# Strassen's seven products for the gate and up projections of a hybrid decoder layer's two FFNs, and the down projection in three batches

## Chip, core and metric

The kernel runs on one core of one Trainium2 chip. The metric is device time in microseconds (us): the median over runs of the whole program. PE is TensorE, DVE is VectorE, ACT is ScalarE, POOL is GpSimd, SP is the engine whose queue issues most DMAs.

## What is computed

One inference step of a layer over 544 tokens (512 prompt rows and 8 x 4 sample rows), width 1024, all in fp32:

```
x += 0.5 * SwiGLU_1(rms(x))            # gate,up: 1024 -> 2 x 2816, down: 2816 -> 1024
h  = rms(x); u = h @ w_in              # mixer: windowed attention and gated DeltaNet
x += merged(attention, deltanet) @ w_out
x += 0.5 * SwiGLU_2(rms(x))
y  = rms(x)
def _swiglu(x, w_gu, w_down):
    gate, up = jnp.split(x @ w_gu, 2, axis=-1)
    return (jax.nn.silu(gate) * up) @ w_down
```

## The kernel before

Channels lie on the partitions, tokens along the free axis, in two halves of 272 (`sl(0)`, `sl(1)`). A product of two fp32 matrices is made of three matmuls of rounded parts: every operand is kept as hi (rounded) and lo (the rest), and `unit` issues hi x hi, hi x lo and lo x hi for each of the 8 tiles of the contraction, 24 matmuls of 128x128 by 128x272 into one PSUM accumulator.

The program is built by Python: `make_plan` writes the list of units, `kernel_units` goes through it. For each unit it calls `prefetch` (which brings weight tiles in), the unit's own function (its matmuls), and then the unit's `evac` (what DVE, ACT and POOL make of the accumulator). Every engine works through its own queue in the order of issue.

An FFN has 22 slices of 128 hidden channels. A slice costs four units: gate (`u_g`) and up (`u_u`) for two token halves, 96 matmuls. `u_g`'s evac multiplies by 1/rms (`R(h)`) on DVE and takes a tanh on ACT; `u_u`'s evac makes silu(gate) * up with three more DVE operations and splits it into `hh` hi (ACT) and lo (DVE). After 11 slices comes a batch of 16 down units (`u_d`, 33 matmuls each) whose evac adds to the residual `x`; then 11 more slices and 16 more down units.

Weights arrive in chunks of 8 tiles (`raw`, 512 KB, SP queue), are split in groups of four tiles (128x512) into hi by ACT and lo by a DVE subtraction (`split_next`; in the mixer the subtraction is mostly POOL's). Outside the mixer there are 8 + 4 such groups (`G2`, `G`), so three slices' worth can be ready ahead. The norm: `xw_tile` multiplies x by the norm's weight and splits it (`xh`, `xl`), `norm_acc` sums squares on POOL, `norm_fin` makes 1/rms on DVE, which is applied after the products.

Of the kernel before, what the change touches and what calls it, by code (L numbers as in the profile page):

```python
# [10 lines left out]
F32 = mybir.dt.float32  # L11
# [14 lines left out]
FB = 11  # L26
# [99 lines left out]
class Plan:  # L126
    """Order in which the 128 x 128 weight tiles are used; host and chip follow it."""
# [16 lines left out]
def stagger(n, tail, head=0):  # L144
    """(tile, half) order: the first `head` and the last `tail` tiles go half by half."""
    out = [(i, h) for h in range(2) for i in range(head)]
    for i in range(head, n - tail):
        out += [(i, 0), (i, 1)]
    out += [(i, h) for h in range(2) for i in range(n - tail, n)]
    return out  # L150


def make_plan():
    pl = Plan()
    units = []

    def ffn(which):
        gu, dn = f"w_ffn{which}_gu", f"w_ffn{which}_down"
        for b in range(2):
            order = stagger(FB, 0, 2 if b == 0 else 0) if (which, b) != (1, 0) else stagger(FB, 2, 2)  # L160
            for f, h in order:
                f += b * FB
                units.append(("g", which, f, h, pl.col(gu, range(KT), f * P)))
                units.append(("u", which, f, h, pl.col(gu, range(KT), (FT + f) * P)))
            for n, h in stagger(KT, 0 if b == 0 else 2 if which == 1 else 4):
                units.append(("d", which, b, n, h, pl.col(dn, range(b * FB, b * FB + FB), n * P)))

# [36 lines left out]
def consts():  # L204
    """Arrays that depend on shapes alone: identity, masks and distances."""
# [53 lines left out]
class Builder:  # L259
    def __init__(self, tc, nc, A, pl, units, cp, sp, pp, dp):  # L260
# [5 lines left out]
        self.next_group = 0  # L266
        self.next_raw = self.top = 0
        self.side = []
        self.due, self.rings = {}, {}
        self.last = False  # L270
        self.busy = set()
        self.nps = 0
        self.in_mix = False
        self.plan_groups()
# [15 lines left out]
    def until(self, ok):  # L290
        """The side chains go on until something holds."""
# [57 lines left out]
    def mm_ps(self):  # L349
        self.nps += 1  # L350
        if not self.in_mix and self.nps % 8 > 2:
            return self.sd_ps()
# [28 lines left out]
    def mm(self, out, lhsT, rhs, start=True, stop=True):  # L381
        return self.nc.tensor.matmul(out, lhsT, rhs, start=start, stop=stop)
# [5 lines left out]
    def rsqrt(self, out, v, tmp, steps):  # L388
        """out = v ** -0.5 by a shifted exponent and Newton steps."""
# [3 lines left out]
        for k in range(steps):  # L393
            a, b = (-0.703952253, 0.703952253 * 2.38924456) if k == 0 else (-0.5, 1.5)
            self.tt(tmp, out, out, ALU.mult)
            self.stt(tmp, tmp, a, v, ALU.mult, ALU.mult)
            self.stt(out, tmp, b, out, ALU.add, ALU.mult)
            yield "vector"

# [1 line left out]
    def load_raw(self, upto):  # L401
        nch = self.A["in_W_dram"].shape[0]
        while self.next_raw <= min(upto, nch - 1):
            c = self.next_raw
            pool, tag, bufs = self.sp, "raw", CFG["RAW"]
            if c % 3 == 2 and not self.in_mix and c * CHUNK // GRP not in self.resident:
                pool, tag, bufs = self.mp, "raw2", 1
# [5 lines left out]
    def plan_groups(self):  # L413
        self.last_use, self.resident = {}, set()
        first_pa = next(i for i, u in enumerate(self.units) if u[0] == "pa")
        first_ba = next(i for i, u in enumerate(self.units) if u[0] == "ba")
        for i, u in enumerate(self.units):
            for t in u[-1]:
                self.last_use[t // GRP] = i
                if first_ba <= i < first_pa:  # L420
                    self.resident.add(t // GRP)
        self.held = {"G": [], "G2": []}

    def split_next(self, ui, pool=None):
        """Bring the next group of weight tiles in as hi + lo if a slot is free."""
        k = self.next_group
        c = k * GRP // CHUNK
        for tag, bufs in (("G2", CFG["G2"]), ("G", CFG["G"])):
            if tag == "G2" and (k in self.resident or self.in_mix):
                continue  # L430
            self.held[tag] = [g for g in self.held[tag] if self.last_use[g] >= ui]
            if len(self.held[tag]) < bufs:
                break
# [1360 lines left out]
```

## Time and profile before

| | |
|---|---|
| median of 3 runs | 1734.03 us (1730.92 to 1737.05) |
| profiled execution, span | 1730.2 us |
| PE / DVE / ACT / POOL busy | 1656.1 / 1072.3 / 573.1 / 373.4 us |
| mean granted TensorE clock | 0.983 |
| first FFN, mixer, second FFN (about) | 8 to 415, 415 to 1285, 1317 to 1717 us |

Busy times are unions of the recorded spans of an engine. A matmul's own span (288 ns) overlaps those of its neighbours, so the cost of one is its pitch, not its span. The median is 3.8 us above the profiled span.

### The profile page before, as it was taken

To read this page: it belongs to the slowest core of one execution; us is meant where nothing else is said; L and a number is where in the kernel's file an instruction comes from. 1 tells how busy PE (TensorE), PEld (TensorE's weight loads), DVE (VectorE), ACT (ScalarE), POOL (GpSimd) and SP (SyncE) were. 2 spreads that over 40 slices of the span, in tenths; PEclk is the share of its full clock that TensorE was granted. 3 is DMA by queue.
4 is the path that set the end of the run, shared out by engine and by line. 5 is a ranking of instruction groups with operands and counts; after the bars stand their busy time and mean duration, and the time that the engine had idled before them with its cause. 6 is when DMAs were issued, how large, how long until landed. Compare 5 with 4: busy or idle time off the path is not lost.

```text
span 1730.2 us, 33573 instructions
## 1 busy us (share of the span) xinstructions
PE 1656.1 (96%) x13373; PEld 1607.8 (93%) x13373; DVE 1072.3 (62%) x2508; ACT 573.1 (33%) x1356; POOL 373.4 (22%) x441
## 2 busy tenths in 40 slices
PE   8999999999988999999899899999999999999997
PEld 7999999999988888888889788999999999999996
DVE  7754255545879869789958665344456654255534
ACT  5332223332332324343333244333233323223332
POOL 5000000011545534454425233420011000000012
PEclk9999999999999999999999999999999999999999
DMA  5223222322333455446347666332243222223221
GB/s 177 87 85 98 86 86 86 98 85 75 111 100 115 135 180 185 135 156 193 117 137 238 171 219 182 123 119 89 86 139 97 84 89 87 97 74 98 86 75 63
DMA packets 116434, 205.13 MB, mean 119 GB/s; under 512 B 30962, under 2 KB 57108, under 8 KB 116276
## 3 DMA queue, kind: packets, MB, share of 16 engines
q1 hardware_dynamic: 104708, 162.43, 29.2%
q0 software_dynamic: 10992, 39.99, 7.7%
q8 instruction: 105, 1.72, 0.4%
q10 hardware_dynamic: 576, 0.56, 0.1%
q14 instruction: 53, 0.43, 0.1%
HBM read 172.20 MB, written 30.73 MB: 117 GB/s over the span
## 4 chain that ended last, share of the span: by engine, by line
PE 73%; DVE 20%; DMA 3%; ACT 2%; issue 2%; SPq 1%; POOL 0%; DVEq 0%; ACTq 0%
PE sd L120 40%; PE mm L120 32%; DVE y L120 4%; DVE Yc L120 3%; DVE inv L120 2%; DVE H L120 1%; DVE nrm L120 1%; DVE ast L120 1%; DVE av L120 1%; DVE s L120 1%; DVE R L120 1%; DMA md<-ast 1%; DVE U L120 1%; DVE kq L120 1%; DVE r L120 1%
## 5 line engine op out<-in xcount | busy, mean ns | idle before, releaser
L120 PE MATMUL mm<-xh,G 128*128 128x272 f32 x3632 | 753.7, 297 | 21.6 <-DVE smp L120 10.4
L120 PEld LDWEIGHTS mm<-xh,G 128*128 128x128 f32 x3632 | 596.6, 192 | 42.5 <-issue 26.5
L120 PE MATMUL mm<-xl,G 128*128 128x272 f32 x1816 | 530.0, 292 | 0.5 <-DVE xl L120 0.4
L120 PE MATMUL sd<-xh,G 128*128 128x272 f32 x1904 | 363.4, 288 | 0.0
L120 PEld LDWEIGHTS mm<-xl,G 128*128 128x128 f32 x1816 | 349.2, 192 | 1.4 <-DVE xl L120 0.6
L120 ACT ACTIVATE G<-raw 128x512 fp32r<-128x512 f32 x474 | 273.3, 619 | 178.6 <-PE mm L120 111.6
L120 PEld LDWEIGHTS sd<-xh,G 128*128 128x128 f32 x1904 | 300.5, 188 | 0.2
L120 POOL TENSOR_TENSOR G<-raw,G 128x512 fp32r<-128x512 f32 x158 | 217.3, 1391 | 322.7 <-ACT G L120 303.0
L120 PE MATMUL sd<-xl,G 128*128 128x272 f32 x952 | 273.8, 288 | 0.0
L120 DVE TENSOR_TENSOR G<-raw,G 128x512 fp32r<-128x512 f32 x316 | 204.7, 690 | 70.9 <-ACT G L120 66.7
L120 POOL TENSOR_TENSOR acc<-acc,H 128x272 f32<-128x272 f32 x55 | 44.7, 814 | 911.5 <-ACT H L120 908.1
L120 PEld LDWEIGHTS sd<-xl,G 128*128 128x128 f32 x952 | 179.0, 188 | 0.1
L120 PE MATMUL sd<-hh,G 128*128 128x272 f32 x1287 | 163.0, 288 | 0.0
L120 PEld LDWEIGHTS sd<-hh,G 128*128 128x128 f32 x1287 | 161.8, 188 | 0.1
L120 ACT ACTIVATE H<-H 128x272 f32<-128x272 f32 (+1 forms) x105 | 45.1, 429 | 193.4 <-DVE H L120 193.4
L120 ACT ACTIVATE hh<-H 128x272 fp32r<-128x272 f32 x88 | 38.0, 431 | 202.0 <-DVE H L120 202.0
L120 PE MATMUL mm<-hh,G 128*128 128x272 f32 x825 | 104.7, 288 | 0.0
L120 PEld LDWEIGHTS mm<-hh,G 128*128 128x128 f32 x825 | 103.8, 188 | 0.0
L120 DVE SCALAR_TENSOR_TENSOR y<-U,vec,y 128x568 f32<-128x568 f32 x72 | 94.2, 1308 | 7.8 <-ACT y L120 6.0
L120 DVE SCALAR_TENSOR_TENSOR H<-H,H 128x272 f32<-128x272 f32 x120 | 55.2, 460 | 26.3 <-ACT H L120 25.8
L120 DVE SCALAR_TENSOR_TENSOR x<-sd,x 128x272 f32<-128x272 f32 x49 | 21.4, 439 | 77.9 <-PE sd L120 77.9
L120 DVE TENSOR_TENSOR hh<-H,hh 128x272 fp32r<-128x272 f32 x88 | 38.9, 442 | 43.8 <-ACT hh L120 43.8
(257 smaller groups left out, 1853.3 us busy)
## 6 DMA issues: line engine op xcount, KB each, us to landing
raw<-in_W_dram SPq DMA_DIRECT2D x161, 512.0 KB, 3.6
raw<-in_W_dram POOLq DMA_DIRECT2D x76, 512.0 KB, 4.0
qkv<-qd SPq DMA_DIRECT2D x36, 256.0 KB, 5.4
st<-in_ssm_dram SPq DMA_DIRECT2D x32, 256.0 KB, 4.5
cache<-in_kc_dram SPq DMA_DIRECT2D x28, 256.0 KB, 5.2
cache<-in_vc_dram SPq DMA_DIRECT2D x28, 256.0 KB, 4.3
qd<-av SPq DMA_DIRECT2D x24, 256.0 KB, 4.2
out_dram<-av SPq DMA_DIRECT2D x24, 256.0 KB, 3.8
```

The costliest lines, as they stand in the source:

```text
L120: r = f(*args, **kw)
```

## The change

Slices 0 to 3 of the first FFN and 0 to 2 of the second stay as they were. The other 18 + 19 = 37 slices are computed as a 2 x 2 x 2 block product: gate and up are the block rows (A1, A2), the lower and upper four contraction tiles the inner blocks, the two token halves the block columns. Seven products (`PROD`; units `"w"`) of four contraction tiles each replace the eight: 7 x 12 = 84 matmuls. Two pairs of them and one triple accumulate in one bank each, and a product's partial sum is read out of the bank before the next product adds to it.

For that, POOL makes four weight sums of 128x512 per slice (`sums`), and four combinations of the blocks of x (T1 to T4, four tiles each) are made once per FFN (`tset`, on DVE, ACT and POOL). Weights are now split in 1024-wide jobs (sums too), 3 x 1024 + 512 columns per slice instead of 4 x 512; all those subtractions are DVE's. 1/rms is no longer multiplied into up, but into the down product. The hidden value is split for both halves at once (544 wide), lo by POOL except in a batch's last slice. Down runs in batches of 8, 7 and 7 slices; its evac multiplies by 1/rms on DVE and adds to x on POOL (DVE in the last batch).

```diff
+PROD = {1: ("A11", "B11", "A", True), 2: ("A12", "B21", "A", False), 6: ("S2", "T2", "B", True), 7: ("S3", "T3", "B", False),
+        4: ("A22", "T4", "B", False), 5: ("S1", "T1", "C", True), 3: ("S4", "B22", "C", False)}
+FBS = (8, 7, 7)
+NC = {1: 4, 2: 3}
...
+            for f in range(max(f0, nc), f0 + n):
+                if (f, 1) not in begun:
+                    w(f, 1)
+                if f > max(f0, nc):
+                    w(f - 1, 4)
+                last = f == f0 + n - 1
+                w(f, *[p for p in (6, 5, 2, 7) + (() if last else (3,)) if (f, p) not in begun])
+            if f + 1 < FT:
+                w(f + 1, 1)
+            w(f, 3, 4)
+            if f + 1 < FT:
+                w(f + 1, 2, 6, 5)
...
+    def sums(self, j):
...
+        if k[0] == "12":
+            self.tt(t[:, h[1]], y[:, h[0]], y[:, h[1]], ALU.add, pg)
+            self.tt(t[:, h[0]], t[:, h[1]], x[:, h[0]], ALU.add, pg)
+            self.s2 = t
+        else:
+            self.tt(t[:, h[0]], x[:, h[0]], y[:, h[1]], ALU.add, pg)
+            self.tt(t[:, h[1]], x[:, h[1]], self.s2[:, h[0]], ALU.add, pg)
...
+    def u_w(self, which, f, p, wids):
...
+            if p == 1:
+                e["p1"] = self.H()
+                self.act(e["p1"], ps, AF.Copy)
+            elif p == 6:
+                e["V"] = self.H()
+                self.tt(e["V"], ps, e["p1"], ALU.subtract)
+            elif p == 5:
+                e["p5"] = self.H()
+                self.act(e["p5"], ps, AF.Copy)
+            elif p == 2:
+                e["g"] = self.S(name="g")
+                self.tt(e["g"][:, h0], ps, self.R(0), ALU.mult)
...
+            elif p == 7:
+                u3 = self.H()
+                self.tt(u3, ps, e["p1"], ALU.subtract)
+                e["u"] = self.S(name="u")
+                self.tt(e["u"][:, h1], u3, e.pop("p5"), ALU.subtract, pg)
+            elif p == 3:
+                t, g = self.H(), e["g"]
+                self.tt(t, ps, e.pop("V"), ALU.subtract)
+                self.tt(g[:, h1], t, self.R(1), ALU.mult)
+                e["t"] = self.S(name="t")
+                self.act(e["t"], g, AF.Tanh, scale=0.5)
+                self.stt(e["t"], e["t"], 1.0, g, ALU.add, ALU.mult)
...
+            else:
+                t, u = e["t"], e["u"]
+                self.tt(u[:, h0], ps, e["p1"], ALU.subtract)
+                self.tt(t, t, u, ALU.mult)
+                self.h[f] = tuple(self.S(dt=F32R, name="hh") for k in range(2))
+                self.split(*self.h[f], t, None if f + 1 in (FBS[0], FBS[0] + FBS[1], FT) else pg)
```

The order on DVE for one slice of the old kind, slice 4 of the first FFN (G<-raw are the lo halves of weights, H and hh the evacuations of gate and up, two halves one after the other):

```order
L120 TENSOR_TENSOR G_797<-raw_568,G_797 128x512
L120 TENSOR_TENSOR G_800<-raw_568,G_800 128x512
L120 TENSOR_TENSOR H_830<-sd_805,r_361 128x272
L120 TENSOR_TENSOR G_834<-raw_667,G_834 128x512
L120 TENSOR_TENSOR G_837<-raw_667,G_837 128x512
L120 SCALAR_TENSOR_TENSOR H_831<-H_831,H_830 128x272
L120 TENSOR_TENSOR H_831<-H_831,r_361 128x272
L120 TENSOR_TENSOR H_831<-H_831,sd_842 128x272
L120 TENSOR_TENSOR hh_868<-H_831,hh_867 128x272
```

The second half follows with five more such operations and no weights. In the change a slice of the new kind (slice 9) has these twelve on DVE, in the order of the products 6, 2, (weights), 7, (weights), 3, (weights of the slice after next), 4:

```order
L130 TENSOR_TENSOR H_2041<-sd_2028,H_2002 128x272
L130 TENSOR_TENSOR g_2072<-mm_1989,r_363 128x272
L130 TENSOR_TENSOR G_2058<-sw_1942,G_2058 128x1024
L130 TENSOR_TENSOR H_2092<-sd_2028,H_2002 128x272
L130 TENSOR_TENSOR G_2078<-sw_1984,G_2078 128x1024
L130 TENSOR_TENSOR H_2111<-sd_2043,H_2041 128x272
L130 TENSOR_TENSOR g_2072<-H_2111,r_492 128x272
L130 SCALAR_TENSOR_TENSOR t_2114<-t_2114,g_2072 128x544
L130 TENSOR_TENSOR G_2120<-raw_1964,G_2120 128x1024
L130 TENSOR_TENSOR u_2094<-sd_2028,H_2002 128x272
L130 TENSOR_TENSOR t_2114<-t_2114,u_2094 128x544
L130 TENSOR_TENSOR G_2138<-raw_1881,G_2138 128x512
```

Seven of the twelve read two tiles in SBUF; five read an accumulator (sd, mm). On POOL, which had nothing to do in this stretch before, the same slice now has these six (sw are the weight sums for slice 11, two slices ahead):

```order
L130 TENSOR_TENSOR sw_2075<-raw_2026 128x512
L130 TENSOR_TENSOR sw_2075<-sw_2075,raw_1964 128x512
L130 TENSOR_TENSOR u_2094<-H_2092,H_2056 128x272
L130 TENSOR_TENSOR sw_2117<-raw_1964,raw_2026 128x512
L130 TENSOR_TENSOR sw_2117<-raw_1964,sw_2075 128x512
L130 TENSOR_TENSOR hh_2155<-t_2114,hh_2154 128x544
```

POOL's work moved from none to six operations a slice. At the start of the first FFN the lo halves of the third slice's weights stood on POOL before, right behind the sums of squares:

```order
L120 TENSOR_TENSOR acc_216<-acc_216,H_236 128x272
L120 TENSOR_TENSOR G_316<-raw_154,G_316 128x512
L120 TENSOR_TENSOR G_319<-raw_154,G_319 128x512
L120 TENSOR_TENSOR G_324<-raw_175,G_324 128x512
L120 TENSOR_TENSOR G_327<-raw_175,G_327 128x512
```

Now they stand on DVE, behind the evacuations of the first two slices and four operations that make half-sums of x (yt):

```order
L130 TENSOR_TENSOR H_384<-H_384,sd_324 128x272
L130 TENSOR_TENSOR hh_388<-H_384,hh_387 128x272
L130 TENSOR_SCALAR yt_445<-x_73,vec_79 128x272
L130 SCALAR_TENSOR_TENSOR yt_445<-x_73,vec_79,yt_445 128x272
L130 TENSOR_SCALAR yt_450<-x_74,vec_79 128x272
L130 SCALAR_TENSOR_TENSOR yt_450<-x_74,vec_79,yt_450 128x272
L130 TENSOR_TENSOR G_418<-raw_159,G_418 128x1024
L130 TENSOR_TENSOR G_458<-raw_172,G_458 128x1024
```

Those weights moved from an engine that was otherwise free of evacuations into the queue that has them.

## Rows read from the trace of the kernel before

**Rows 1.** The page: span, and busy time of each engine (share, instructions).

```profile
span 1730.2 us, 33573 instructions
PE 1656.1 (96%) x13373; PEld 1607.8 (93%) x13373; DVE 1072.3 (62%) x2508; ACT 573.1 (33%) x1356; POOL 373.4 (22%) x441
```

**Rows 2.** Windows: us, then PE, PEld, DVE, ACT, POOL busy, PEclk, DMA, GB/s.

```profile
8.07:150.80 142.73, 138.38 (x1062) 136.94 (x1063) 96.78 (x182) 53.51 (x118) 21.20 (x20) 0.98 0.33 108
150.80:216.80 66.00, 66.00 (x530) 66.00 (x529) 20.79 (x39) 14.82 (x25) 0.00 (x0) 1.00 0.28 89
216.80:349.10 132.30, 132.30 (x1059) 132.30 (x1058) 75.46 (x153) 40.50 (x85) 0.00 (x0) 1.00 0.28 88
415.00:1285.00 870.00, 816.80 (x6759) 772.74 (x6759) 614.66 (x1615) 298.52 (x787) 318.18 (x373) 0.97 0.46 146
1486.00:1620.00 134.00, 134.00 (x1070) 134.00 (x1069) 67.46 (x136) 37.63 (x76) 0.00 (x0) 1.00 0.29 91
```

**Rows 3.** Chain of work that ended last, one of its longest pieces: start, us, what.

```profile
66.66 15.04 PE sd L120 x120
```

**Rows 4.** Groups by form: busy us, mean ns of one, idle before.

```profile
L120 DVE TENSOR_TENSOR G<-raw,G 128x512 fp32r<-128x512 f32 x316 | 204.7, 690 | 70.9 <-ACT G L120 66.7
L120 DVE TENSOR_TENSOR hh<-H,hh 128x272 fp32r<-128x272 f32 x88 | 38.9, 442 | 43.8 <-ACT hh L120 43.8
L120 DVE TENSOR_TENSOR H<-sd,r 128x272 f32<-128x272 f32 x65 | 28.6, 440 | 35.8 <-PE sd L120 35.7
L120 ACT ACTIVATE G<-raw 128x512 fp32r<-128x512 f32 x474 | 273.3, 619 | 178.6 <-PE mm L120 111.6 <-PE sd L120 43.7 <-DMA raw<-in_W_dram 12.1
L120 ACT ACTIVATE hh<-H 128x272 fp32r<-128x272 f32 x88 | 38.0, 431 | 202.0 <-DVE H L120 202.0
```

**Rows 5.** Tiles acc and G, POOL's instructions: duration ns min/median/max.

```profile
L120 POOL TENSOR_TENSOR acc<-acc,H x55: 767/775/1265, 13.7 to 1714.5; 128x272 f32<-128x272 f32 x55
L120 POOL TENSOR_TENSOR G<-raw,G x158: 1260/1289/1927, 9.5 to 1145.3; 128x512 fp32r<-128x512 f32 x158
```

**Rows 6.** Timeline of DVE, 242 us: start, us, instruction, count.

```profile
242.47 1.29 DVE L120 TENSOR_TENSOR G<-raw,G 128x512 fp32r<-128x512 f32 x2
```

**Rows 7.** Timeline of POOL, 13 to 34 us.

```profile
13.69 13.93 POOL L120 TENSOR_TENSOR acc<-acc,H 128x272 f32<-128x272 f32 x14
27.57 5.68 POOL L120 TENSOR_TENSOR G<-raw,G 128x512 fp32r<-128x512 f32 x4
```

**Rows 8.** Timeline of DVE, 25 to 42 us.

```profile
25.96 0.42 DVE L120 TENSOR_SCALAR H<-sd 128x272 f32<-128x272 f32 x1
...
27.88 1.34 DVE L120 TENSOR_TENSOR H<-r 128x272 f32<-128x272 f32 x1
29.26 1.41 DVE L120 SCALAR_TENSOR_TENSOR H<-H,H 128x272 f32<-128x272 f32 x1
30.70 1.42 DVE L120 SCALAR_TENSOR_TENSOR r<-H,r 128x272 f32<-128x272 f32 x1
32.16 1.40 DVE L120 TENSOR_TENSOR H<-r 128x272 f32<-128x272 f32 x1
33.59 0.44 DVE L120 SCALAR_TENSOR_TENSOR H<-H,H 128x272 f32<-128x272 f32 x1
...
35.60 0.44 DVE L120 SCALAR_TENSOR_TENSOR H<-H,H 128x272 f32<-128x272 f32 x1 [0.56 <-ACT H L120]
...
40.72 0.44 DVE L120 TENSOR_TENSOR hh<-H,hh 128x272 fp32r<-128x272 f32 x1 [0.49 <-ACT hh L120]
41.08 0.43 DVE L120 TENSOR_SCALAR H<-mm 128x272 f32<-128x272 f32 x1
```

**Rows 9.** Timeline of PE, 35 to 38 us.

```profile
35.20 1.06 PE L120 MATMUL mm<-acc,mats 128*128 128x272 f32 x2 [2.53 <-DVE H L120]
37.05 0.59 PE L120 MATMUL mm<-xh,G 128*128 128x272 f32 x1 [0.79 <-DVE H L120]
```

**Rows 10.** DMA issues: KB each, median us to landing.

```profile
raw<-in_W_dram SPq DMA_DIRECT2D x161, 512.0 KB, 3.6
```

More of the change, by code (lines that the diff above doesn't have):

```diff
@@ L155, in make_plan, with gu_tiles, w @@
     units = []
+    def gu_tiles(which, f):
+        gu = f"w_ffn{which}_gu"
+        g, u = f * P, (FT + f) * P
+        x = [pl.tid(gu, k, g) for k in range(KT)]
+        return lambda: (x, [pl.tid(gu, k, u) for k in (4, 5, 6, 7, 0, 1, 2, 3)])
     def ffn(which):
         gu, dn = f"w_ffn{which}_gu", f"w_ffn{which}_down"
[L159 to L166, printed above, removed]
+        at, begun = {}, set()
+        def w(f, *ps):
+            if f not in at:
+                at[f] = gu_tiles(which, f)()
+            for p in ps:
+                begun.add((f, p))
+                units.append(("w", which, f, p, [("W", at[f], PROD[p][0])]))
+        nc = NC[which]
+        for f, h in stagger(nc, 0, 2):
+            if f not in at:
+                at[f] = pl.col(gu, range(KT), f * P), pl.col(gu, range(KT), (FT + f) * P)
+            if (f, h) == (nc - 1, 1):
+                w(nc, 1)
+            for k in range(2):
+                units.append(("gu"[k], which, f, h, at[f][k]))
+        f0 = 0
+        for b, n in enumerate(FBS):
+            for f in range(max(f0, nc), f0 + n):
[10 more added lines that the diff above has]
+                w(f + 1, 2, 6, 5)
+            for m, h in stagger(KT, 0 if b < 2 else 4):
+                units.append(("d", which, b, m, h, pl.col(dn, range(f0, f0 + n), m * P)))
+            f0 += n
     def gates(n):
@@ L402, in load_raw, with chunks, load_raws @@
+    @staticmethod
+    def chunks(k):
+        return k[1:] if len(k) == 3 else [k[1]] if k[0] == "c" else [k[1] * GRP // CHUNK]
+    def load_raws(self):
         nch = self.A["in_W_dram"].shape[0]
-        while self.next_raw <= min(upto, nch - 1):
+        while self.next_raw < nch:
             c = self.next_raw
-            pool, tag, bufs = self.sp, "raw", CFG["RAW"]
-            if c % 3 == 2 and not self.in_mix and c * CHUNK // GRP not in self.resident:
-                pool, tag, bufs = self.mp, "raw2", 1
+            for pool, tag, bufs in ((self.sp, "raw", CFG["RAW"]), (self.mp, "raw2", CFG["RAW2"])):
+                if tag == "raw2" and (self.in_mix or c in self.resident):
+                    continue
+                if len(self.raw_live[tag]) < bufs:
+                    break
+            else:
+                return
+            self.raw_live[tag].add(c)
@@ L424, in split_next, with read_raw @@
-    def split_next(self, ui, pool=None):
[L426 to L433, printed above, removed]
-        else:
+    def read_raw(self, k):
+        for c in self.chunks(k):
+            self.reads[c] -= 1
+            if not self.reads[c]:
+                del self.raws[c]
+                for live in self.raw_live.values():
+                    live.discard(c)
@@ L435, in split_next @@
+    def split_next(self, ui, pool=None):
+        j = self.next_job
+        k = self.jobs[j]
+        tag, bufs, w = ("G", CFG["G"], 512) if k[0] == "g" else ("W2", CFG["W2"], 1024)
+        if tag == "W2" and self.in_mix:
+            return False
+        self.held[tag] = [g for g in self.held[tag] if self.last_use[g] >= ui]
+        if len(self.held[tag]) >= bufs:
+            return False
+        self.load_raws()
+        if any(c not in self.raws for c in self.chunks(k)):
             return False
@@ L650, in kernel_units @@
     def kernel_units(self):
-        nu = len(self.units)
-        self.h = {}
-        self.gsum = {}
+        self.early = {3: (0, 1), 5: (2, 3)}
+        self.tsets = {8 + 2 * n: (0, (4 + n,)) for n in range(4)}
+        i = next(i for i, u in enumerate(self.units) if u[0] == "g" and u[1] == 2)
+        for n in range(4):
+            self.tsets[i + 1 + n // 2] = 2, range(n // 2 * 2, n // 2 * 2 + 2)
+            self.tsets[i + 4 + 2 * n] = 2, (4 + n,)
+        self.h, self.ev, self.bank = {}, {}, {}
         pend = []
@@ L657, in kernel_units @@
             pend.append(getattr(self, "u_" + u[0])(*u[1:]))
+            for n in self.early.get(ui, ()):
+                self.tset(n, 0)
             if ui in (3, 6):
+                self.do_los()
                 self.norm_fin(ui // 3 - 1)
```

284 lines of the change are left out of this document (211 added, 73 removed).

## The prediction

> **What bounds the kernel now.** I read the page first: PE is busy 96% of the span [rows 1]. Then the windows by stage: inside both FFNs PE is busy without a gap at full granted clock, while DVE works 57% (first FFN) or 50% (second) of a stretch of gate and up units and POOL does nothing at all [rows 2]; only the mixer has PE gaps (816.8 of 870 us), and the change leaves its work alone. So in the FFNs time is matmuls times pitch. The chain's longest pieces give the pitch: 120 matmuls in 15.04 us, 0.1253 us each [rows 3]; 1059 in 132.3 us says the same [rows 2]. Then I looked for what POOL's idleness has been sparing DVE, since the change gives POOL work there. At 27.6 to 33.3 us both work at once: POOL does four 128x512 subtractions in 5.68 us, 1.42 us each [rows 7], and DVE's 272-wide operations with two SBUF inputs, 0.44 us by themselves, take 1.34 to 1.42 us, one per POOL operation; the moment POOL ends, DVE is back at 0.44 [rows 8]. An operation that reads an accumulator in the same time keeps its 0.42 us [rows 8]. So two-input DVE operations and POOL's tensor operations take turns. A pair costs 1.42 us where 1.29 + 0.44 = 1.73 stand alone [rows 4, 5, 7]: about 0.3 us of each pair overlaps.
>
> The Trainium skill says of this (SBUF — State Buffer, section Who interferes with whom) that a DVE instruction with two SBUF inputs and a GpSimd instruction that reads SBUF exclude each other for the whole instruction. The trace agrees that they take turns, but the turn is 0.3 us shorter than the two durations together; the rule to the letter is rival C below.
>
> **What is removed.** A new slice has 84 matmuls for 96: 10.5 us for 12.0 at the pitch above. 37 slices x 12 = 444 matmuls, 444 x 0.1253 = 55.6 us off PE if nothing else ends later.
>
> **What a new slice asks of DVE and POOL.** DVE prices: 272 wide 0.44, 512 wide 0.69 [rows 4]; from these two, 1.03 ns a column, so 544 wide 0.72 and 1024 wide 1.22 by estimate (two 512s back to back, 1.29, bound it above [rows 6]). POOL: 272 wide 0.78, 512 wide 1.29 [rows 5], so 544 wide 1.36 by estimate.
> - DVE, two SBUF inputs: 3 x 1.22 + 0.69 (weights) + 0.44 + 2 x 0.72 = 6.2 us. DVE, from accumulators: 5 x 0.44 = 2.2. With the wait for the tanh between two of them (0.56 at half the width [rows 8]; I take 0.75 at 544) and some 0.45 of gaps, DVE alone needs 9.6 us: it would fit under 10.5.
> - POOL: 4 x 1.29 (sums) + 0.78 + 1.36 = 7.3 us.
> - Taking turns: 6.2 + 7.3 - 6 x 0.3 = 11.7 us a slice, more than PE's 10.5. It gets there only if POOL works in all of DVE's 3.4 us without a two-input operation (2.2 + 0.75 + 0.45). Walking down the order shown above it doesn't: the sums start when a chunk has landed (3.6 us after its issue [rows 10], and the issue waits for the lo half that frees its buffer), which puts them against the run of weights, g x r, silu, weights, t x u, weights; and POOL has nothing ready while DVE does the cheap reads of products 6 and 2. About 2.6 of the 3.4 is used, so I take **12.5 us a slice** in the steady state. PE cannot run ahead of this: product 7 adds to the bank that DVE reads as V, product 4 to the one that it reads as u3, two products (3.0 us) after each is done.
>
> What is left of ACT fits: 3 x 1.02 + 0.62 (weights, scaled from 0.43 and 0.62 [rows 4]), two copies of 0.43, tanh and hi of 0.64 each: 5.8 us. The raw chunks come 1 MB per slice, as before.
>
> **Per stage.** A stage of 7 slices is not all steady state: of its 28 sums, 8 are issued in the down units before it, where POOL has only 0.78 us per unit of 2.6 to 3.0 us. Sums of the change's own POOL and DVE rows: in the second stage of an FFN 20 sums stand, in the third 18 and fewer weights (the next slices' are not there). So second stage: 7 x 12.5 - 8 x 1.0 - 0.7 = 78.8 us, third: 87.5 - 10 x 1.0 - 1.9 = 75.6, both against 84.0 before and a PE floor of 73.5. First stage: 4 slices, 10 sums for 16: 50 - 6 + 1 = 45 for 48; in the second FFN 5 slices: 57.5 for 60. Sum: 2 x 154.4 + 45 + 57.5 = 411 us for 444, **-33 us**.
>
> **The start of each FFN.** There DVE and POOL get T1 to T4 as well: 16 POOL operations of 0.78 and on DVE 16 two-input ones and 4 scalings (about 8.5 us), on top of the first sums (8 x 1.29). In the first FFN I count 45 us of two-input DVE work and 33 of POOL's until the first new slice, where PE has 16 units x 24 x 0.1253 = 48 us. Also the third slice's weights now wait behind the evacuations of the first two (eight operations from about 34.6 to 41 us [rows 8]), while its unit is due at about 36. For it: 1/rms is ready sooner without POOL's four subtractions in its way, and PE already lost 2.53 + 0.79 us at this place [rows 9]. Bounds 0 and 15 us; I take **+8**, and **+4** for the second FFN, whose sums of squares come earlier.
>
> **Hidden.** Down: the same 1056 matmuls per FFN; 16 more evacuations of 0.44 us, under units of 2.6 us or more; if that cover were gone, 16 x 0.44 x 2 = 14 us. The add to x (0.78 on POOL, 0.44 on DVE in the last batch) lies under the next unit but for the last, +0.5 us. One multiplication per half-slice (88 x 0.44) leaves DVE and is worth nothing where PE bounds. The mixer's matmuls are the same but issued in another order, since the order follows an estimate of the engines' times: -8 to +8, taken as 0.
>
> **Sum.** 1730.2 - 33 + 8 + 4 + 0.5 = 1710 us of span. The runs' median lies 3.8 above the profiled span, so **1714 us**, 1.2% faster.
>
> **Rivals.**
> A. PE stays the bound: DVE lags behind PE only by what the two-product distance and the two slices of sums made ahead absorb, so that a stage runs near 10.5 us a slice. For it: DVE by itself needs 9.6, and the second stage's turns add up to 73 to 74 us against 73.5 on PE. Against it: it needs a perfect interleaving. -55.6 + 5 at the starts: about 1684. Chance 0.20.
> B. The forecast, 1700 to 1728: 0.50.
> C. The turns are worse than the pairs in the trace: POOL, always with something queued, gets in ahead of every weight subtraction, and the V and u3 reads come late, so that PE waits in each slice. The price is the slice time T: the stages take 37 T - 50 us and the starts 12, so beyond T = 13.0 the kernel is slower than before. With nothing overlapping T is 6.2 + 7.3 = 13.5: 37 x 13.5 - 50 + 12 - 444 = +17, 1751. By the skill's rule to the letter T is this 13.5. For it: every two-input operation of DVE from 27.9 to 33.6 us waited for a whole POOL operation [rows 8]. Against it: the same rows' overlap, and the sums moved into the down units. Chance 0.18.
> D. The gain in the slices is there, but the starts (15 + 8) and the mixer's other order eat it: within 5 us of 1734. Chance 0.12.
>
> **Numbers.** A measurement of this kernel tells about 0.3% (5 us) from no change. Faster by more than that: A and B, 0.70; same: D, 0.12; slower: C, 0.18. The range runs from A's 1684 to just below C's centre: 1683 to 1746 leaves out the faster tail of A and the upper half of C. B's own range is 1700 to 1728.
>
> **What would show it.** Windows over the second stages of 7 slices: PE busy below 100% (10.5 of about 11.3 us), DVE above 85%, POOL above 50%; 75 to 80 us per stage for A's 73.5 and C's 85. DVE's weight subtractions of 1024 columns longer than 1.22 us on average, in the range of 1.5 to 2.5 where POOL works, accumulator reads still 0.44. PE waiting for DVE's H (V, u3) or G tiles, not for raw or POOL. At the first FFN's third slice a PE wait of some us for G. In the down stages PE without gaps. The forecast is wrong if PE is gapless in the slices (A), if a slice takes over 13 us (C), or if the mixer's 870 us move by more than 10.

## The result, and the profile after

The changed kernel takes 1762.11 us (median of four runs, 1755.41 to 1763.55) where the kernel before took 1733.86 beside it: a ratio of 1.0155, 95% interval 1.0124 to 1.0187. It is slower by 1.6%; the forecast was 1.2% faster. The profiled execution has a span of 1761.0 us, 30.8 above the one before.

First the page, which answers to [rows 1]: PE does 55 us less of matmuls (444 fewer) in a longer span, and DVE and POOL are busier.

```profile
span 1761.0 us, 32895 instructions
PE 1625.8 (92%) x12929; PEld 1567.2 (89%) x12929; DVE 1254.9 (71%) x2453; ACT 633.8 (36%) x1304; POOL 813.1 (46%) x748
```

PE loses only 30 us of busy time for 55.6 us of matmuls, mostly since more of them run at a lower granted clock (mean 0.972, 0.983 before), last longer there and count as busy; more on that below. Then the chain that ended last by engine, before and after (the page's part 4): DVE's share goes from a fifth to a third.

```profile
PE 73%; DVE 20%; DMA 3%; ACT 2%; issue 2%; SPq 1%; POOL 0%; DVEq 0%; ACTq 0%
```

```profile
PE 50%; DVE 35%; issue 6%; ACT 5%; DMA 3%; POOL 1%; SPq 0%; DVEq 0%; ACTq 0%; POOLq 0%
```

What PE waits for (after: us in total, times, longest). The first line is new; the second is the mixer's, as before (10.4).

```profile
PE sd L130 <- DVE H L130: 49.3, 28, 4.3
PE mm L130 <- DVE smp L130: 10.6, 4, 5.1
```

H after an sd bank is what DVE makes of V and u3, the two sums that PE must not overwrite; "smp" is a tile of the mixer. Windows of the changed kernel, columns as in [rows 2]: the first down units, the second stage (7 slices), the third, and the second stage of the second FFN; then three stretches of the first FFN's start.

```profile
134.02:182.10 48.08, 48.08 (x387) 48.08 (x386) 19.12 (x28) 9.41 (x10) 25.89 (x21) 1.00 0.33 110
182.10:264.40 82.30, 75.10 (x591) 73.99 (x590) 71.87 (x82) 36.17 (x54) 55.03 (x36) 1.00 0.22 78
306.40:383.00 76.60, 69.25 (x543) 68.14 (x543) 67.21 (x77) 33.22 (x50) 52.83 (x34) 1.00 0.27 92
1498.50:1581.20 82.70, 75.22 (x591) 74.09 (x590) 72.25 (x82) 36.16 (x54) 55.02 (x36) 1.00 0.22 77
...
40.00:48.00 8.00, 7.87 (x47) 7.49 (x48) 6.97 (x12) 3.52 (x6) 2.60 (x2) 0.79 0.17 45
64.00:72.00 8.00, 4.33 (x23) 3.89 (x22) 7.40 (x14) 5.37 (x11) 3.29 (x5) 0.72 0.17 58
96.00:104.00 8.00, 5.47 (x32) 5.47 (x33) 6.76 (x7) 2.83 (x4) 5.36 (x4) 0.79 0.38 131
```

In the second stage DVE is busy 87% and POOL 67% of the time. PE has 588 matmuls there, 73.7 us at the pitch of [rows 3], and the stage lasts 82.3. PE's timeline in it shows how (start, us, what, count, and the wait in brackets): one wait of 1.3 to 1.6 us in each slice but the first and the last, always before product 7, which adds to the bank that DVE reads as V (the 24 matmuls are products 7 and 3).

```profile
194.33 3.28 PE L130 MATMUL sd<-bs,G 128*128 128x272 f32 x24 [1.58 <-DVE H L130]
...
206.74 3.27 PE L130 MATMUL sd<-bs,G 128*128 128x272 f32 x24 [1.60 <-DVE H L130]
...
218.86 3.28 PE L130 MATMUL sd<-bs,G 128*128 128x272 f32 x24 [1.35 <-DVE H L130]
...
231.02 3.28 PE L130 MATMUL sd<-bs,G 128*128 128x272 f32 x24 [1.35 <-DVE H L130]
```

One slice on DVE, from one read of V (218.38) to the next (230.53): 12.15 us. Every operation follows the one before without a gap, but for the wait for the tanh.

```profile
218.38 0.43 DVE L130 TENSOR_TENSOR H<-sd,H 128x272 f32<-128x272 f32 x1
218.73 0.43 DVE L130 TENSOR_TENSOR g<-mm,r 128x272 f32<-128x272 f32 x1
219.08 1.68 DVE L130 TENSOR_TENSOR G<-sw,G 128x1024 fp32r<-128x1024 f32 x1
220.68 0.43 DVE L130 TENSOR_TENSOR H<-sd,H 128x272 f32<-128x272 f32 x1
221.03 1.21 DVE L130 TENSOR_TENSOR G<-sw,G 128x1024 fp32r<-128x1024 f32 x1
...
222.66 1.07 DVE L130 TENSOR_TENSOR g<-H,r 128x272 f32<-128x272 f32 x1
224.45 1.01 DVE L130 SCALAR_TENSOR_TENSOR t<-t,g 128x544 f32<-128x544 f32 x1 [0.73 <-ACT t L130]
225.40 1.78 DVE L130 TENSOR_TENSOR G<-raw,G 128x1024 fp32r<-128x1024 f32 x1
227.11 0.43 DVE L130 TENSOR_TENSOR u<-sd,H 128x272 f32<-128x272 f32 x1
227.65 1.27 DVE L130 TENSOR_TENSOR t<-t,u 128x544 f32<-128x544 f32 x1
228.84 1.77 DVE L130 TENSOR_TENSOR G<-raw,G 128x512 fp32r<-128x512 f32 x1
230.53 0.43 DVE L130 TENSOR_TENSOR H<-sd,H 128x272 f32<-128x272 f32 x1
```

POOL in the same time:

```profile
217.87 1.80 POOL L130 TENSOR_TENSOR hh<-t,hh 128x544 fp32r<-128x544 f32 x1
222.14 1.29 POOL L130 TENSOR_TENSOR sw<-raw 128x512 f32<-128x512 f32 x1 [2.47 <-DMA raw<-in_W_dram]
223.51 1.37 POOL L130 TENSOR_TENSOR sw<-sw,raw 128x512 f32<-128x512 f32 x1
224.84 1.26 POOL L130 TENSOR_TENSOR u<-H,H 128x272 f32<-128x272 f32 x1
226.07 2.27 POOL L130 TENSOR_TENSOR sw<-raw,raw 128x512 f32<-128x512 f32 x1
228.30 1.76 POOL L130 TENSOR_TENSOR sw<-raw,sw 128x512 f32<-128x512 f32 x1
```

Put the two side by side. From 219.7 to 222.1 POOL waits for the next chunk, and there DVE's 1024-wide subtraction takes 1.21 us. From 222.1 on POOL has work without a break, and the same subtraction takes 1.78, the 512-wide one 1.77 (0.69 by itself, [rows 4]), silu 1.01 and t x u 1.27 (each 0.73 in the kernel without sums below). That is the turn-taking of [rows 8], now in every slice. The reads of an accumulator keep their 0.43. POOL stands idle 2.3 to 2.5 us in such a slice, waiting for the chunk; no run lets the chunk land earlier, so what that would give is open. The groups by form of DVE give the mean over the kernel (busy us, mean ns of one, idle before):

```profile
L130 DVE TENSOR_TENSOR G<-raw,G 128x1024 fp32r<-128x1024 f32 x121 | 177.1, 1464 | 11.9 <-ACT G L130 11.9
L130 DVE TENSOR_TENSOR G<-sw,G 128x1024 fp32r<-128x1024 f32 x74 | 106.2, 1436 | 5.1 <-ACT G L130 5.1
L130 DVE TENSOR_TENSOR G<-raw,G 128x512 fp32r<-128x512 f32 x43 | 52.9, 1233 | 1.1 <-ACT G L130 1.1
L130 DVE TENSOR_TENSOR H<-sd,H 128x272 f32<-128x272 f32 x111 | 48.2, 434 | 11.2 <-PE sd L130 11.2
```

The Trainium skill (SBUF — State Buffer, section Who interferes with whom) says that a DVE instruction with one SBUF input at most, outside the 2-port performance modes, does not contend with GpSimd, and that one with two SBUF inputs contends with a GpSimd instruction that reads SBUF. The four rows agree: 0.434 us for the accumulator reads, undisturbed, and 1.23 to 1.46 for the others.

**Where 30.8 us come from.** By PE's timeline the first FFN (to the mixer's first matmul) goes from 415.1 to 426.9 us, +11.8; the mixer (to the last w_out matmul) from 902.2 to 908.7, +6.5; the second FFN to the end from 412.9 to 425.4, +12.5. In each FFN, against the pitch:

| us | first FFN | second FFN |
|---|---|---|
| matmuls left out (18 and 19 slices x 12 x 0.1253) | -27.1 | -28.6 |
| first stage, time above its matmuls: 10.4 before, 28.0 after (768 matmuls in 124.2 us); 2.2 (whole FFN) before, 20.2 after | +17.6 | +18.0 |
| second stage (588 matmuls, 73.7 us) | +8.6 | +9.0 |
| third stage (540 matmuls, 67.7 us) | +8.9 | +8.8 |
| PE's first matmul later; last down units and tail | +3.7 | +5.7 |
| sum (measured: 11.8 and 12.5) | 11.7 | 12.9 |

So nothing of the matmuls' time comes back: some two thirds of it go to PE's waits in the second and third stages, and as much again to the starts.

### The profile page after: what moved, and what is told of

Its sections match the earlier page's. It is cut to its first block, busy times and chain, and to the rows that moved or that the text cites. A ratio compares the mean times of both kernels' runs of the same rounds, so it can differ in the third digit from the quotient of the medians.

```text
span 1761.0 us, 32895 instructions
## 1 busy us (share of the span) xinstructions
PE 1625.8 (92%) x12929; PEld 1567.2 (89%) x12929; DVE 1254.9 (71%) x2453; ACT 633.8 (36%) x1304; POOL 813.1 (46%) x748
## 3 DMA queue, kind: packets, MB, share of 16 engines
q8 instruction: 101, 1.65, 0.4%
## 4 chain that ended last, share of the span: by engine, by line
PE 50%; DVE 35%; issue 6%; ACT 5%; DMA 3%; POOL 1%; SPq 0%; DVEq 0%; ACTq 0%; POOLq 0%
PE sd L130 26%; PE mm L130 24%; DVE G L130 9%; DVE H L130 4%; DVE y L130 3%; DVE Yc L130 3%; DVE inv L130 2%; DVE g L130 2%; ACT G L130 2%; DMA md<-ast 1%; DVE nrm L130 1%; DVE r L130 1%; DVE ast L130 1%; DVE av L130 1%; DVE R L130 1%
## 5 line engine op out<-in xcount | busy, mean ns | idle before, releaser
L130 PE MATMUL mm<-xh,G 128*128 128x272 f32 x2560 | 548.1, 302 | 19.4 <-DVE smp L130 10.6
L130 PEld LDWEIGHTS mm<-xh,G 128*128 128x128 f32 x2560 | 426.7, 194 | 39.0 <-issue 27.7
L130 PE MATMUL sd<-bs,G 128*128 128x272 f32 x2676 | 359.5, 292 | 49.1 <-DVE H L130 45.0
L130 PEld LDWEIGHTS sd<-bs,G 128*128 128x128 f32 x2676 | 346.5, 191 | 56.3 <-DVE H L130 50.3
L130 PE MATMUL mm<-xl,G 128*128 128x272 f32 x1280 | 374.9, 293 | 0.1
L130 ACT ACTIVATE G<-raw 128x512 fp32r<-128x512 f32 (+1 forms) x316 | 241.8, 785 | 175.0 <-PE mm L130 110.3
L130 DVE TENSOR_TENSOR G<-raw,G 128x1024 fp32r<-128x1024 f32 (+1 forms) x164 | 229.9, 1404 | 13.0 <-ACT G L130 13.0
L130 PE MATMUL mm<-bs,G 128*128 128x272 f32 x1104 | 158.6, 295 | 9.4 <-ACT G L130 5.4
L130 PEld LDWEIGHTS mm<-bs,G 128*128 128x128 f32 x1104 | 148.4, 194 | 12.3 <-ACT G L130 6.4
L130 DVE TENSOR_TENSOR G<-sw,G 128x1024 fp32r<-128x1024 f32 x74 | 106.2, 1436 | 5.1 <-ACT G L130 5.1
```

The source lines that it names most:

```text
L130: r = f(*args, **kw)
```

## The experiments

The theory: DVE's operations with two SBUF inputs and POOL's operations take turns, their work on a slice (with T sets at the start, more) is more than PE's 10.5 us, and so it is a question of how much of it falls into a stretch. The rivals: another part of the change costs the time; DVE is too full by itself; a new slice has a chain of waits of its own that costs 1.65 us wherever it stands. All kernels are timed against runs of the kernel before on the same chip. "FFN 1", "mixer" and "FFN 2" are the three parts as above, from each kernel's profiled execution.

| kernel | median us | ratio to before, 95% interval | FFN 1, mixer, FFN 2 |
|---|---|---|---|
| before (first trace) | 1733.86 | 1 | 415.1, 902.2, 412.9 |
| the change | 1762.11 | 1.0155 [1.0124, 1.0187] | 426.9, 908.7, 425.4 |
| no sums | 1693.57 | 0.9767 [0.9733, 0.9802] | 399.9, 898.0, 391.4 |
| three batches only | 1736.91 | 1.0019 [1.0001, 1.0038] | 415.6, 901.5, 416.0 |
| two sums on DVE | 1748.03 | 1.0075 [1.0053, 1.0097] | 421.3, 901.9, 417.4 |
| third slice's lo on POOL | 1765.12 | 1.0176 [1.0141, 1.0212] | 429.4, 904.4, 425.7 |
| interleaved | 1724.83 | 0.9938 [0.9916, 0.9960] | 406.3, 909.0, 407.3 |
| every other slice | 1740.43 | 1.0018 [1.0001, 1.0035] | 414.0, 911.0, 411.2 |
| two of three slices | 1728.89 | 0.9955 [0.9940, 0.9969] | 411.1, 910.9, 406.4 |
| interleaved, later start | 1717.83 | 0.9888 [0.9858, 0.9918] | 403.5, 913.0, 401.0 |
| interleaved, five first, batches of 5 and 4 | 1719.58 | 0.9908 [0.9874, 0.9942] | 410.5, 912.1, 400.5 |
| later start, estimates reset | 1714.26 | 0.9880 [0.9848, 0.9911] | 403.3, 914.2, 401.0 |
| interleaved, six first | 1710.69 | 0.9840 [0.9809, 0.9872] | 401.7, 910.3, 397.3 |
| interleaved, five first | 1715.25 | 0.9870 [0.9837, 0.9903] | 410.5, 905.3, 396.6 |

**No sums.** The four POOL sums of a slice go; the weights are split from a raw chunk, by the same instructions on ACT and DVE.

```diff
-        for i in range(j, j + 4):
-            self.sums(i)
         if len(k) == 3:
-            src = self.sw.pop(k)
+            src = self.raws[k[1 if k[0] == "12" else 2]]
```

> Leaves out the four weight sums that POOL makes per new slice (the raw weights are split in their place, so the FFN outputs are not the reference's); every DVE, ACT and PE operation stays. In the changed kernel a new slice repeats every 12.15 us. Theory A (DVE's two-input operations and POOL's operations take turns, and that sets the slice): without 4 x 1.29 us of POOL a slice falls to near PE's 10.5 us, the 7-slice stage from 82.4 to 74 to 76 us, the kernel by 37 x 1.3 to 1.6 us plus something at the starts: 1695 to 1710 us. Theory B (PE waits because a product adds to a bank that DVE reads, a chain of latencies whatever POOL does): slices stay at 12.1, kernel within 10 us of 1762. Theory C (DVE simply has too much to do, 9.6 us and more): slices at 11.5 or more, 1735 to 1762.

Measured: 1693.57 us, 68 less than the change. The window over its second stage, with the same 82 DVE instructions:

```profile
172.70:246.40 73.70, 73.70 (x591) 73.70 (x591) 54.19 (x82) 37.56 (x54) 20.31 (x14) 1.00 0.28 93
```

PE is gapless at its floor of 73.7 us. DVE's busy time falls from 71.87 to 54.19 us with nothing taken from DVE: 17.7 us of its time in the stage was waiting for POOL, inside its instructions. By form, the 1024-wide subtraction is back at its price by itself (my estimate was 1.22):

```profile
L130 DVE TENSOR_TENSOR G<-raw,G 128x1024 fp32r<-128x1024 f32 x195 | 239.3, 1227 | 19.0 <-ACT G L130 19.0
...
L130 DVE TENSOR_TENSOR t<-t,u 128x544 f32<-128x544 f32 x37 | 26.9, 726 | 4.2 <-DVE u L130 0.5
```

So the waits in the slices are POOL's sums, by way of DVE, and DVE without them fits, as the prediction's 9.6 us per slice had it. It also shows what the block products are worth where the sums are not in their way: 1733 - 1694 = 39 us of the 55.6.

The starts keep a loss without the sums. By PE's timeline the first stages take 18.9 and 4.7 us above their matmuls here, 28.0 and 20.2 in the change. In the first FFN three long waits of the change (4.29 us before 39.95, 1.88 and 1.79 us before 66.89 and 69.19) are still there, and only what comes later is gone (4.12 us before 98.53, 1.86 before 112.59):

```profile
39.64 1.07 PE L130 MATMUL sd<-acc,mats 128*128 128x272 f32 x2 [4.28 <-DVE H L130]
...
65.67 0.51 PE L130 MATMUL mm<-bs,G 128*128 128x272 f32 x2 [1.89 <-ACT G L130]
67.98 2.63 PE L130 MATMUL mm<-bs,G 128*128 128x272 f32 x10 [1.80 <-DVE G L130]
```

So of the 17.6 us that the first FFN's start lost, about 9 are the sums'; of the second's 18.0, about 15. (Each is the difference of the two times above the matmuls.)

**Three batches only.** The rest of the change without block products: every slice an old one, no T sets and no sums, down in batches of 8, 7 and 7.

```diff
-            for f in range(max(f0, nc), f0 + n):
...
+            for f, h in stagger(n, 0, 2 if b == 0 else 0):
...
-        names = ("B11", "B21", "B12", "B22", "T1", "T2", "T3", "T4")
+        names = ("B11", "B21", "B12", "B22")
```

> One part of the change alone: all 22 slices in the old form (96 matmuls), but down in batches of 8, 7 and 7 slices, 1/rms moved from up to down, weights in 1024-wide jobs in four buffers, x split into blocks; no block products. The result stays the reference's. If the loss is all in the new slices (A): within 6 us of the kernel before, 1728 to 1742. If the batches, the smaller weight buffers or the mixer's other order cost by themselves: 1743 or more. The mixer's stretch (902 us in the kernel before from the last down unit to the last w_out unit, 912 in the changed one) shows how much of that part is due to order alone.

Measured: 1.0019 [1.0001, 1.0038], 3.9 us, hardly to be told from no change. The time from the last down matmul to the end is 17.3 us here as in the change, 13.6 before: the longer tail belongs to the shorter last batch (7 slices for 11; with 6 it takes 17.3 to 18.7 us in the kernels below, with 5 18.8, with 4 19.8). Of the rest of the 28 us nothing shows here: the mixer takes 901.5 us, and the first stages lie 8.8 and 1.0 us above their matmuls, so what the starts keep without the sums comes with the T sets and the first new slices; no run separates these two. (The changed kernel's mixer, counted as in the expectation, takes 908.5 us, not 912.)

**Two sums on DVE.** S3 and S4 move from POOL to DVE.

```diff
-            self.tt(t[:, h[0]], x[:, h[0]], y[:, h[1]], ALU.add, pg)
-            self.tt(t[:, h[1]], x[:, h[1]], self.s2[:, h[0]], ALU.add, pg)
+            self.tt(t[:, h[0]], x[:, h[0]], y[:, h[1]], ALU.add)
+            self.tt(t[:, h[1]], x[:, h[1]], self.s2[:, h[0]], ALU.add)
```

> Moves two of the four weight sums of a slice (the pair S3, S4) from POOL to DVE, result unchanged. DVE gets 2 x 0.69 us more per slice, POOL loses 2 x 1.29. Theory A (turns): the sum of the turns falls by 1.2 us a slice (11.7 to 11.1 with one overlap less per POOL operation), so a slice takes 11.3 to 12.0 us and the kernel 1735 to 1757. Theory C (DVE's own load decides): slices 1.0 to 1.4 us longer, 1790 to 1810. Theory B: 1762 within 8.

Measured: 1748.03, 14 us less than the change. The second stage:

```profile
180.00:260.90 80.90, 75.40 (x591) 74.09 (x591) 67.86 (x92) 36.19 (x54) 35.87 (x26) 1.00 0.22 79
```

DVE was given ten operations more and is busy 4 us less; POOL's 55.03 become 35.87. An engine that is too full by itself would have become slower. What is saved is the difference in price, 0.69 for 1.29 us [rows 4, 5], in a shared turn. It is little: a slice takes 12.0 us for 12.15, at the upper end of theory A's 11.3 to 12.0. In the profiled execution, 20 us shorter than the change's, the four later stages gain 7.5 us, the starts 5.8 and the mixer 6.8.

**Third slice's lo on POOL.** For the weights that are split at units 3 to 7, DVE's subtraction goes to POOL.

```diff
-            if not self.split_next(ui):
+            if not self.split_next(ui, True if 3 <= ui < 8 else None):
```

> Gives POOL back the lo halves of the weights that are split while the first tiles of the first FFN run (units 3 to 7), as the kernel before had it; result unchanged. The changed kernel's first stage takes 124 us to the first down unit where 103 us of slices stand in it. If the third slice's weights behind DVE's evacuations cost the start: 4 to 8 us less, 1754 to 1758, the 4.6 us PE wait at 35 us and the waits at 57 to 69 us shorter. If DVE and POOL as a whole are overfull there: within 3 us of 1762, as the work only changes hands.

Measured: 1765.12, the same as the change. The loss at the start isn't the third slice's place in DVE's queue. That the stretch is too full as a whole fits this, but is not shown by it.

**Interleaved.** If it is a matter of throughput, the down units are the place for the sums: there DVE is busy 19.12 and POOL 25.89 of 48.08 us (first window above). All 37 slices stay; down comes in five batches, and four down units stand behind every slice. 1/rms is multiplied into silu(gate) again, one more 544-wide DVE operation a slice, which makes a down evacuation one operation again.

```diff
-FBS = (8, 7, 7)
+FBS = (4, 4, 4, 4, 6)
+DG = 4
...
+        for f in range(nc, FT):
...
+            w(f, 6, 5, 2, 7, 3)
+            if f in ends[:-1]:
+                down += [(ends.index(f), m, h) for m, h in stagger(KT, 0)]
+            downs(DG)
```

> All 37 block-product slices stay, but down comes in five batches (4, 4, 4, 4, 6) and four down units of a finished batch stand behind every block-product slice, so that sums and weight subtractions have the down matmuls (10.5 us per slice at 0.1253) to spread over; 1/rms is multiplied into the up sum, so that a down evacuation is one operation again. Theory A (a slice takes 12.15 us because the two-input work of DVE and POOL, 6.2 + 7.3 less the overlap, does not fit in 10.5 us; what does not fit waits in turn, and it is only a matter of throughput): with 10.5 us of down work behind each slice it fits, PE stalls in the slices go, and the time is near 1733 - 55.6 + 10 to 20 at the starts and the tail, 1685 to 1705. Rival E (each slice has a local chain of waits, weights to product to evacuation over two products, that costs its 1.65 us whatever stands beside it): slices still take 12.1, and the time is about 1750 to 1760.

Measured: 1724.83, faster than before by 0.6% and than the change by 2.1%. Windows over the interleaved part of each FFN (second and fourth line), and over the starts:

```profile
41.00:90.30 49.30, 42.23 (x291) 41.01 (x290) 42.93 (x70) 22.08 (x40) 25.91 (x22) 0.87 0.18 55
129.30:344.35 215.05, 215.05 (x1718) 215.05 (x1717) 162.50 (x235) 85.05 (x117) 120.09 (x79) 1.00 0.28 96
1324.87:1388.60 63.73, 52.55 (x376) 51.21 (x375) 56.44 (x82) 25.54 (x46) 37.34 (x30) 0.92 0.18 58
1421.50:1642.50 221.00, 221.00 (x1766) 221.00 (x1765) 168.18 (x242) 86.63 (x119) 119.66 (x81) 1.00 0.29 99
```

PE has no wait in 215 and in 221 us of block products with down units, though each slice has the same sums, the same weights, and instructions that still slow each other (the 1024-wide subtractions take 1.38 and 1.56 us on average in the first of the two). The down units stand behind product 3 and not between 6 and 7, where the waits were, so a local chain of 1.65 us per slice is out. The time missed the 1685 to 1705 that I gave it: the mixer took 7 us more than before, the tail 4, and the starts were not touched: 288 matmuls took 49.3 us there and 372 took 63.7, 13 and 17 above the pitch, DVE busy 87 to 89% and the granted clock down to 0.87 and 0.92.

**Every other slice, and two of three.** Old slices (no sums) stand between the new ones; down as in the change, in batches of 8, 8 and 6.

```diff
+def old(f):
+    return f % 2 == 1
...
+                if old(f):
+                    for h in range(2):
+                        for k in range(2):
+                            units.append(("gu"[k], which, f, h, at[f][k]))
```

(`f % 3 == 0` in the second.)

> Behind the first four slices of each FFN every second slice is an old one (gate and up as 96 matmuls, no sums, no T): 18 block-product slices for 37; down in batches of 8, 8 and 6. Theory A: a pair asks 11.7 of turns for the new slice and about 6.9 us of DVE alone for the old one, 18.6 us against 22.5 of PE, so PE stalls inside the pairs go and each new slice gives its whole 1.5 us: 18 x 1.5 = 27 off, and with 10 to 20 at the starts and tail 1716 to 1726 (windows over the middle of a stage: PE busy about 100%, 22.5 us per pair). Rival E (the 1.65 us wait is local to a new slice): a pair takes 24.1, nothing is gained, 1740 to 1755.

> As the kernel with every second slice old, but only every third one is: 24 block-product slices. Theory A: a triple asks 2 x 11.7 + 6.9 = 30.3 us of turns against 33.0 of PE; it fits, with little to spare, so between the full 24 x 1.5 = 36 us off and half of it: 1705 to 1730. Rival E: a triple takes 36.3, and the time is 1745 to 1760.

Measured: 1740.43 and 1728.89. The second stages (720 matmuls, 90.2 us by the pitch; 708, 88.7):

```profile
176.50:267.90 91.40, 90.68 (x724) 90.46 (x723) 63.26 (x88) 35.11 (x54) 32.53 (x22) 1.00 0.30 93
```

```profile
176.40:266.20 89.80, 89.08 (x710) 88.86 (x709) 65.88 (x90) 36.56 (x56) 41.84 (x28) 1.00 0.29 93
```

A pair takes 22.9 us (22.5 expected, 24.1 by the rival), so a new slice gives most of its 1.5 us once turns have room. The total of the first is 14 us above its range all the same: its mixer takes 911.0 for 902.2, its first stages are 20.2 and 7.4 us above their matmuls, and 18 slices only pay for that. The second is within its range.

**Later start.** What is left is the start. Six old slices stand first for four and three, and the work on the T sets is spread over every fourth unit (the edit is shown against the interleaved kernel; the second FFN's T sets move likewise).

```diff
-FBS = (4, 4, 4, 4, 6)
+FBS = (6, 4, 4, 4, 4)
...
-NC = {1: 4, 2: 3}
+NC = {1: 6, 2: 6}
...
-        self.tsets = {8 + 2 * n: (0, (4 + n,)) for n in range(4)}
+        self.tsets = {8 + 4 * n: (0, (4 + n,)) for n in range(4)}
```

A second kernel has five first, with the T sets on every third unit. In both, and in the next one, batches of 6 or 5 shift the later weight tiles against the chunks, so the later slices use other blocks of the weights than the reference; number and shape of the operations stay.

> The interleaved kernel, with six old slices at the front of each FFN for four and three, the work on the T sets spread over every fourth unit, and down batches of 6, 4, 4, 4, 4: 32 block-product slices. In the interleaved kernel the later slices are gapless, and the loss sits at the starts: 372 matmuls took 63.75 us where the pitch gives 46.6 in the second FFN (17 lost), and about 16 in the first. Theory A (a start is overfull with T sets, first sums and weights at once, a matter of throughput over that stretch): spread out, most of 33 comes back, 5 slices x 1.5 = 7.5 are given up: 1702 to 1716. Rival F (the T sets stand on the path wherever they stand): the loss stays and the slices given up cost: 1728 to 1735.

> As the kernel with six old slices first, with five, the T sets every third unit and down batches of 5, 4, 4, 4, 5: 34 block-product slices. Theory A: 3 us less given up than with six, but less room for the T sets: 1703 to 1720. Rival F: 1726 to 1732.

Measured: 1717.83, 2 us above theory A's range, and 1719.58, at the upper end of its range; both lie 6 to 10 us under rival F's. Spread out, part of the start's loss comes back, though the fewer new slices and the spacing of the T sets were changed together. The mixer took 913.0 us in the first, 4 more than in the interleaved kernel, which that range had not in it.

**Estimates reset.** The order of the mixer's work follows an estimate of each engine's time that the program's planner keeps. At the mixer's start it is cut to TensorE's, to see whether a lead left from the FFN sets the order (the edit is shown against the later start).

```diff
+        m = self.nc
+        now = m.t["tensor"]
+        m.t = {k: min(v, now) for k, v in m.t.items()}
```

> As the kernel with six old slices first, but at the start of the mixer the planner's estimate of each engine's time is set to at most TensorE's. In all versions with block products the mixer (first to last matmul of the projections) took 733 to 740 us, in the kernel before and with two sums on DVE 726. Theory M (the mixer's order depends on the lead that the estimates of DVE and POOL have left from the FFN): about 726 again, 7 us less than the kernel with six first. Rival (the order is the same or any other): within 8 us either way of that kernel, with no sign known.

Measured: 1714.26, not to be told from the kernel that it was made from, and the mixer 914.2 us. The theory on the mixer falls.

**Six and five first, batches of four.** The later start with the interleaved kernel's batches.

```diff
-FBS = (6, 4, 4, 4, 4)
+FBS = (4, 4, 4, 4, 6)
...
-            if f in ends[:-1]:
-                down += [(ends.index(f), m, h) for m, h in stagger(KT, 0)]
+            while done < len(ends) - 1 and ends[done] <= f:
+                down += [(done, m, h) for m, h in stagger(KT, 0)]
+                done += 1
```

> The interleaved kernel (down batches of 4, 4, 4, 4, 6) with six old slices first in each FFN, the work on the T sets on every fourth unit, four down units behind each of the 16 block-product slices. Beside the kernel with batches of 6, 4, 4, 4, 4 only the batches differ. Theory A (a start is overfull as a stretch): the starts lose about 8 and 5 us as there, for 13 and 17 in the interleaved kernel with four and three first; 7.5 us of block products are given up: 1710 to 1720. Rival F (the T work stands on the path wherever it is put): 1728 to 1735.

> The same with five old slices first and the T sets on every third unit (17 block-product slices per FFN). Theory A: 3 us less given up than with six, and a fuller start: 1710 to 1722. Rival F: 1726 to 1732.

Measured: 1710.69, 0.984 [0.981, 0.987], which beats both kernels (1.6% and, by the two ratios, 3.1%); with five first 1715.25. Six first, the starts (480 matmuls, 60.1 us by the pitch; 576, 72.2) and the page:

```profile
40.30:108.40 68.10, 64.50 (x483) 63.51 (x482) 57.24 (x95) 29.45 (x52) 26.29 (x22) 0.95 0.25 74
...
1321.50:1398.10 76.60, 74.40 (x579) 74.13 (x578) 59.82 (x104) 31.18 (x56) 27.12 (x24) 0.98 0.24 74
```

```profile
PE 1619.8 (95%) x12989; PEld 1569.2 (92%) x12989; DVE 1212.2 (71%) x2527; ACT 630.9 (37%) x1294; POOL 699.6 (41%) x658
```

The starts lose 8.0 and 4.4 us, for 13 and 17 in the interleaved kernel.

With five first the second FFN is as good (396.6 us, 397.3 with six), but the first takes 410.5 in both kernels with five, more than with four (406.3) or six (401.7). One wait stands in it that neither of those has, for an evacuation that DVE does behind T work:

```profile
84.17 0.79 PE L131 MATMUL mm<-bs,G 128*128 128x272 f32 x2 [4.83 <-DVE H L131]
```

Throughput alone would put five between four and six. So where the T work stands in DVE's queue counts as well, and the account of the starts is not closed.

## Why the prediction was wrong

- **The mechanism** was right: turns between DVE's two-input operations and POOL, PE waiting for V (in the second and third stages never for u3), accumulator reads at 0.43, DVE above 85% and POOL above 50%, down units without gaps. So was the price by itself: 12.15 us a slice for my 12.5, and 1.23 us for the 1024-wide subtraction.
- **The step that failed first** is "a stage of 7 slices is not all steady state": 8.7 and 11.9 us off a stage, 8 and 10 of them for sums issued in the down units before. Measured, the second stage takes 82.3, and the third 76.6 with 48 of its 588 matmuls already done before the down units: 82.6. Seven slices at 12.15 are 85.0, so the deduction is 2.5 us. Each sum that was ready early I had counted as 1.0 us off the stage. But a slice cannot go under PE's 10.5: the first slice runs at 10.5 and wins 1.65, the last makes no sums for a next one, and no lead can be carried further, as there are two sum buffers, which hold one slice's sums. In the down units DVE stands idle for 60% of the time and is given no more. Four stages, the better price of a slice counted: 21 us.
- **The starts**, +8 and +4 within 0 to 15, came to 14.7 and about 14 (the first stages, 124.2 and 114.9 us, less what the other terms gave them): at the upper end of the bounds for the first. I had looked for the one late slice, but no wait for its G came (PE waited 4.29 us for DVE's H there), and giving its weights back to POOL changed nothing. About 9 and 15 us of the loss went with the sums; the rest of the first FFN's came with the T sets and the first new slices, and what of it is throughput and what is place in a queue stays open. The granted clock was lower beside the long waits (0.72 to 0.79 above). That makes 17.
- **The tail**, +0.5, came to +3.6: the add to x in the last unit was priced, the shorter last batch ahead of the norm's sum of squares was not. With later starts of PE and the last down units, 9 in all.
- **The mixer**, 0 within 8, came to +6.5. It is 898 to 902 us in four of the kernels above and 904 to 914 in the others, with the same matmuls; what sets that was not found. A lead of the estimates isn't it.
- **The sum**: 1710 of span forecast; 21 + 17 + 9 - 0.5 + 6.5 more is 1763, measured 1761.0.
- **The rivals.** The sign is C's, but not its way: a slice took less than the 13.0 from which C was to decide. That point came out of 37 T - 50, the same deduction. With the measured 10 for 50, and for the starts the 22 us by which their nine new slices took more than 12.15 each, 37 T - 10 + 22 = 444 gives T = 11.7: even at my sum of turns without any loss the change would have gained nothing. The measured 12.15 stands between PE's 10.5 and the 13.5 of the two engines' times in full: most of them, not all, add up. By the Trainium skill's rule to the letter (SBUF — State Buffer, section Who interferes with whom) it would be the 13.5; no slice here shows that.

## What to carry to other kernels

Work that takes turns with another engine is, less some overlap (here 12.15 us for 13.5), a sum over both engines, and it has to be held against the bound of each stretch, no longer than the buffers can carry a lead: here two sum buffers, one slice: 2.5 us of a stage. Before a stage is filled to its limit, look for the stage beside it that is half empty and mix the two: the same instructions, between down units, left PE without a wait in 215 us. What has to be ready before the first unit of the new kind (the T sets) belongs into the same count, at the place where it is made.

## What the runs showed of the hardware

Who pays in a turn depends on who comes first. With sums, DVE's 1024-wide subtraction takes 1.46 us and POOL's operations are longer too. Without them DVE is back at 1.23, while POOL's 272-wide subtraction (0.775 us is the price of an operation of that width in [rows 5]) takes longer still: in all 37 cases DVE's 1024-wide subtraction had begun 0.23 to 0.26 us before it, while with the sums it mostly met silu, already under way:

```profile
L130 POOL TENSOR_TENSOR u<-H,H 128x272 f32<-128x272 f32 x37 | 48.9, 1321 | 15.4 <-DVE H L130 15.4
```

```profile
L130 POOL TENSOR_TENSOR u<-H,H 128x272 f32<-128x272 f32 x37 | 59.8, 1616 | 92.5 <-DVE H L130 92.5
```

(The change, then the kernel without sums.) And waits of 1.3 to 1.6 us, one in 12 us, leave the granted clock at 1.00 (second stage), while those of 4.29 us before 39.95 us, of 1.88 and 1.79 in a row before 66.89 and 69.19 us, and of 4.12 us before 98.53 us stand beside 0.79, 0.72 and 0.79 in the windows above, means of stretches at 2.4 and at 1.2 GHz. So matmul time was lost beside the long waits as well, and not beside the short ones in the steady slices.
